# A pinned order for the projection's first half, later reads in the v stage and a later norm broadcast in an fp32 encoder on one core

## The chip, the core and the metric

The kernel runs on one core of a Trainium2 chip. The metric is the device time of one execution in microseconds (us), the median of several. The core has TensorE (PE: matmuls, and weight loads shown apart as PEld), VectorE (DVE), ScalarE (ACT), GpSimd (POOL) and SyncE (SP), which here issues DMAs. Each engine takes its instructions in order and waits on semaphores for the others. PSUM, into which PE writes, has eight banks of 128 x 512 fp32. The profile gives PE's granted clock as a share of full speed.

## The reference

An encoder trunk of 1024 tokens by 1024 channels in fp32, with two layers. Layer 0 mixes tokens by attention (16 query heads, 4 key/value heads of 64, with RMS-normalised and rotated queries and keys), layer 1 by a gated spatial unit (gMLP). Each layer ends in an MLP with a squared ReLU. Every part is normalised and modulated by a condition vector:

```python
for i in range(DEPTH):
    mod = cond @ ada_w[i] + ada_b[i]
    sh1, sc1, g1, sh2, sc2, g2 = jnp.split(mod, N_MOD, axis=-1)
    h = modulate(rmsnorm(x, norm1_g[i]), sh1, sc1)
    y = gqa_attention(h, ...) if i % 2 == 0 else chunked_gmlp(h, ...)
    x = x + g1[:, None, :] * y
    h = modulate(rmsnorm(x, norm2_g[i]), sh2, sc2)
    x = x + g2[:, None, :] * sq_relu_mlp(h, mlp_w_in[i], mlp_w_out[i])
```

with `modulate(h, s, c) = h * (1 + c) + s`. In the attention, `qkv = h @ w_qkv`, then the norm and the rotation of q and k, then a softmax per block of 128 queries.

## The kernel before

**Numbers.** Every fp32 operand of a large product is split in a high part (rounded to the engine's fast fp32 format, by ScalarE) and a low part (the difference, by VectorE or GpSimd). A product is then three matmuls: high by high, high by low, low by high. "A split" below is such a pair.

**Head, and the projection of the first 512 tokens.** `x` is held transposed, as eight tiles of 128 channels by 512 tokens (k = 0 to 7) for each half of the tokens. The head broadcasts the condition vector over the partitions by two products (`cb`), sums the squares of the eight tiles (ScalarE squares, VectorE adds), and contracts the sum over the partitions by four narrow products (`ss`, L269). From it `ms` (L271) and a reciprocal root on GpSimd (`r`) are made; `norm_rb` puts the root on a diagonal and multiplies it with ones (`rb`, L284), which broadcasts it over the partitions. Meanwhile the modulation is made for one channel tile at a time: `mod_load` loads a 128 x 1024 tile of `ada_w` and VectorE multiplies and sums it against the condition (L149). Shift and scale are two such tiles per k. `norm_u` multiplies x by scale and root (L293), `norm_hl` adds the shift and splits (L299 on ScalarE, L301 on VectorE).

The projection has three blocks of 512 output columns (cb 0: keys and values, cb 1 and cb 2: queries), with eight k each. `qkv_w(cb, kp, eng)` loads the weights for two k (512 KB), has ScalarE cast the high part (L544) and `eng` subtract the low part (L549). `qkv_mm(cb, kp, ...)` issues 12 matmuls for each k (L558 to L560), into four PSUM banks (two tiles of two banks, or four single banks). Blocks 0 and 1 run pair by pair in the order (0,0), (1,0), (0,1), (1,1), (0,2), (0,3), (1,2), (1,3), then block 2. Block 1's low parts for kp = 0 and block 2's for kp = 0 are made on GpSimd. A scheduler may move instructions where nothing holds them; `hold` keeps an instruction in program order while the flag `pinned` is set, and that is the case only for the first two k.

**Between the halves.** The norm of the second 512 tokens (`norm_rstd(sq1)`: ss, the root, rb) follows the third pair of block 2, with eight of its matmuls between ss and rb as scheduled. `norm_apply` then makes the eight splits of the second half (`hs1`). Keys are rotated and scaled in `k_rows`, which makes the sums of squares (`qk_sums`: square on ScalarE, reduce on VectorE, L606) and the reciprocal root (`qk_rstd`, which takes a square root on ScalarE) before the scaling; `q_sums` is the same for queries. Rotation (`qk_rope`, L616 to L619) reads block 2's banks directly for its queries, so that these banks are free only when it has read them. The second half runs block 0 (into four single banks), block 1 (into the two tiles of block 2 of the first half), then block 2; `kstacks` transposes the split keys on PE (L663).

**MLP and v stage.** The MLP's first product and the gMLP's value product (`wino_v`) use a seven-product scheme on 2 x 2 blocks. Its right operand (weights) and left operand (the normalised x) are combined into "forms", named 1, 2, 6, 5, 7, 3, 4 (`prep` for the weights of the v stage; `forms_b` for x of the second 512 tokens, L366 to L377), and each form is split (L318 and L319 for x, L1463 and L1464 for weights). The work goes in units of 12 matmuls; a callback `at(i)` after unit i issues a piece of other work. In `mlp`, `at` issues ss at unit HB, and rb and `forms_b` one unit later. In the v stage, q names the product and kt its four quarters; `done` reads the banks when a q is through (L1492); two sets of four banks alternate, q5 writing to the banks of q2. In `forms_b(..., apart=True)` the subtractions of the left operand are one step (`subtract`), issued as one run of eight (L377). `prep` makes q6 from three subtractions (L1458 to L1461), of which the third changes the block that q3 uses later.

## Time and profile before

| | |
|---|---|
| median of 3 runs | 2642.19 us (2641.83 to 2645.12) |
| profiled execution, its own time | 2640.55 us |
| its span, first to last instruction | 2638.8 us |
| PE busy | 2597.3 us, 98% |
| VectorE / ScalarE / GpSimd busy | 2183.3 / 1451.1 / 729.8 us |
| mean granted clock of PE | 0.997 |

In the rows shown later, a line of the timeline is start, duration, engine, source line, operation, output tile, input tiles, shape and count, with the idle time before it and the engine, tile and line that ended it in brackets. A row of the grouped waits is the waiting tile and line, the releaser, the total in us, the count, and the longest. Matmuls overlap, so that a matmul's own 0.39 us is longer than the distance to the next.

### The profile page before, as it was taken

To read this page: it belongs to the slowest core of one execution; us is meant where nothing else is said; L and a number is where in the kernel's file an instruction comes from. 1 tells how busy PE (TensorE), PEld (TensorE's weight loads), DVE (VectorE), ACT (ScalarE), POOL (GpSimd) and SP (SyncE) were. 2 spreads that over 40 slices of the span, in tenths; PEclk is the share of its full clock that TensorE was granted. 3 is DMA by queue.
4 is the path that set the end of the run, shared out by engine and by line. 5 is a ranking of instruction groups with operands and counts; after the bars stand their busy time and mean duration, and the time that the engine had idled before them with its cause. 6 is when DMAs were issued, how large, how long until landed. Compare 5 with 4: busy or idle time off the path is not lost. (4 is left out here: it accounts for less than half of the span.)

```text
span 2638.8 us, 37172 instructions
## 1 busy us (share of the span) xinstructions
PE 2597.3 (98%) x12788; PEld 2165.1 (82%) x12788; DVE 2183.3 (83%) x3271; ACT 1451.1 (55%) x2616; POOL 729.8 (28%) x535
## 2 busy tenths in 40 slices
PE   7999999999999999999999999999999999999999
PEld 5788999887788888888788888888888788888887
DVE  7868999887899989977886677788979977789974
ACT  4569999954654455446543444455456645465442
POOL 0238776533000004430122044551520000005400
PEclk9999999999999999999999999999999999999999
DMA  8110222234486788644243355558741554488461
GB/s 288 43 33 1 81 81 80 99 112 144 151 299 244 260 308 301 208 130 171 75 136 112 120 173 179 188 188 307 247 139 49 176 176 153 159 298 276 147 209 60
DMA packets 208751, 435.38 MB, mean 165 GB/s; under 512 B 23025, under 2 KB 35441, under 8 KB 208562
## 3 DMA queue, kind: packets, MB, share of 16 engines
q1 hardware_dynamic: 181682, 395.24, 44.2%
q10 hardware_dynamic: 26880, 37.76, 4.0%
q8 instruction: 101, 1.65, 0.3%
q14 instruction: 88, 0.72, 0.1%
HBM read 310.23 MB, written 122.68 MB: 164 GB/s over the span
## 5 line engine op out<-in xcount | busy, mean ns | idle before, releaser
L1171 PE MATMUL out<-t,s 128*128 128x512 f32 x1232 | 480.1, 390 | 1.4 <-ACT t L318 0.6
L1172 PE MATMUL out<-t,s 128*128 128x512 f32 x1232 | 479.5, 389 | 0.7 <-DVE t L319 0.7
L1173 PE MATMUL out<-t,s 128*128 128x512 f32 x1232 | 479.1, 389 | 0.0
L454 PE MATMUL w<-t,s 128*128 128x512 f32 x1168 | 459.8, 395 | 0.0
L455 PE MATMUL w<-t,s 128*128 128x512 f32 x1168 | 454.8, 390 | 1.5 <-DVE t L319 1.5
L456 PE MATMUL w<-t,s 128*128 128x512 f32 x1168 | 454.6, 389 | 0.0
L319 DVE TENSOR_TENSOR t<-t,t 128x512 fp32r<-128x512 f32 x408 | 329.5, 818 | 32.7 <-ACT t L318 22.4
L318 ACT CAST t<-t 128x512 fp32r<-128x512 f32 x408 | 244.7, 616 | 121.3 <-DMA t<-hf 64.0
L1171 PEld LDWEIGHTS out<-t,s 128*128 128x128 f32 x1232 | 231.2, 188 | 51.1 <-ACT t L318 2.1
L1172 PEld LDWEIGHTS out<-t,s 128*128 128x128 f32 x1232 | 231.2, 188 | 50.1 <-DVE t L319 1.8
L1173 PEld LDWEIGHTS out<-t,s 128*128 128x128 f32 x1232 | 231.2, 188 | 48.2
L439 ACT CAST s<-w 128x512 fp32r<-128x512 f32 x292 | 173.7, 616 | 162.2 <-PE w L456 107.4
L455 PEld LDWEIGHTS w<-t,s 128*128 128x128 f32 x1168 | 219.4, 188 | 48.4 <-DVE t L319 3.7
L454 PEld LDWEIGHTS w<-t,s 128*128 128x128 f32 x1168 | 219.3, 188 | 48.2 <-issue 3.5
L456 PEld LDWEIGHTS w<-t,s 128*128 128x128 f32 x1168 | 219.3, 188 | 45.5
L440 DVE TENSOR_TENSOR s<-w,s 128x512 fp32r<-128x512 f32 x292 | 220.8, 763 | 42.3 <-ACT s L439 41.7
L1153 ACT CAST s<-t 128x512 fp32r<-128x512 f32 x240 | 148.0, 621 | 193.3 <-PE out L1173 139.1
L1139 POOL TENSOR_TENSOR w<-w,t 128x512 f32<-128x512 f32 x20 | 32.4, 1622 | 775.7 <-DMA t<-hf 415.6
L1154 DVE TENSOR_TENSOR s<-t,s 128x512 fp32r<-128x512 f32 x240 | 193.7, 808 | 59.1 <-ACT s L1153 58.4
L910 DVE TENSOR_REDUCE mx<-s 128x1 f32<-128x1024 f32 x128 | 156.2, 1220 | 32.9 <-PE s L907 31.6
L933 DVE TENSOR_TENSOR t<-t,t 128x512 fp32r<-128x512 f32 x256 | 164.2, 682 | 15.9 <-ACT t L927 15.1
L943 PE MATMUL o<-t,t 128*128 128x256 f32 x1024 | 162.7, 291 | 0.0
(248 smaller groups left out, 5086.7 us busy)
## 6 DMA issues: line engine op xcount, KB each, us to landing
t<-hf SPq DMA_DIRECT2D x320, 256.0 KB, 3.7
hf<-c SPq DMA_DIRECT2D x156, 256.0 KB, 3.4
w<-in_wi_dram SPq DMA_DIRECT2D x64, 512.0 KB, 4.4
hf<-c ACTq DMA_DIRECT2D x96, 256.0 KB, 2.3
w<-in_ada_dram SPq DMA_DIRECT2D x36, 512.0 KB, 3.4
x<-in_ada_dram SPq DMA_DIRECT2D x64, 256.0 KB, 5.6
t<-in_wm_dram SPq DMA_DIRECT2D x64, 256.0 KB, 4.7
wf<-w SPq DMA_DIRECT2D x64, 256.0 KB, 2.9
```

The costliest lines, as they stand in the source:

```text
L318: S.copy(hi, src)
L319: (eng or V).tensor_tensor(lo, src, f32(hi), ALU.subtract)
L439: S.copy(hi, src)
L440: V.tensor_tensor(lo, src, f32(hi), ALU.subtract)
L454: T.matmul(ps, hi[:, a], th, start=kt == 0, stop=False)
L455: T.matmul(ps, hi[:, a], tl, start=False, stop=False)
L456: T.matmul(ps, lo[:, a], th, start=False, stop=kt == 3)
L933: pin(V.tensor_tensor(lo, pt, f32(hi), ALU.subtract))
L1154: V.tensor_tensor(lo, src, f32(hi), ALU.subtract)
L1171: T.matmul(ps, hi[:, a], th, start=begin and kt == 0, stop=False, **g)
L1172: T.matmul(ps, hi[:, a], tl, start=False, stop=False, **g)
L1173: T.matmul(ps, lo[:, a], th, start=False, stop=end and kt == 3, **g)
```

## The change

It has three parts.

1. **Head and first half.** `stay(n, src)` issues n products of a 128 x 128 block of ones with a 128 x 128 block of `src` into a bank that nobody reads (36 in all: before `cb`, after the squares of k = 2, 4 and 6, before and after `rb`). Everything from there to the second half's start stands in program order on PE, VectorE and ScalarE. The loop goes over single k, and for k below 6 multiplies block 0 and block 1 in turn; block 1's k = 6 and 7 follow later. All low parts of the first half's weights are made on VectorE. The loads of the modulation for k+1 are issued during k, into buffers named by `MT` (tag w or c). The second half's squares are spread over the first half; ss is issued in the middle of block 2's third pair, rb 24 matmuls later, with the diagonal made by one VectorE product. `k_rows` is divided: the rotation of the keys stands ahead of `norm_apply`; their sums, root and scaling (`k_scale`), and the sums and roots of block 1's queries, stand behind it. In the second half `k_scale` stands behind the first key transposes.
2. **MLP of layer 0.** rb and `forms_b` are issued two units after ss (`HR`), not one.
3. **v stage.** For the first third of the columns (p = 0) the third subtraction of q6 is put in a list and issued after unit 13, and the reads of q2's banks after units 9 to 11. The left operand's subtractions are divided between the forms 5 and 4, at whose split they are now made; the units at which pieces of `forms_b` are issued change, and the statistics begin after unit 15 instead of 13.

PE's order at the start of the program shows the unread products (`dm`). Before:

```order
1 L676 MATMUL cb_111<-c_91,ones 128x512
2 L676 MATMUL cb_113<-c_91,ones 128x512
3 L269 MATMUL ss_147<-ones,t_116 128x1 x4
4 L284 MATMUL rb_168<-t_156,ones 128x512
5 L558 MATMUL qkv_194<-s_160,t_174 128x512
```

With the change:

```order
1 L695 MATMUL dm_111<-ones 128x128 x10
2 L702 MATMUL cb_122<-c_91,ones 128x512
3 L702 MATMUL cb_124<-c_91,ones 128x512
4 L695 MATMUL dm_135<-t_132,ones 128x128 x6
5 L695 MATMUL dm_148<-t_145,ones 128x128 x6
6 L695 MATMUL dm_161<-t_158,ones 128x128 x4
7 L274 MATMUL ss_177<-ones,t_127 128x1 x4
8 L695 MATMUL dm_206<-ones 128x128 x6
9 L289 MATMUL rb_213<-t_186,ones 128x512
10 L695 MATMUL dm_215<-ones 128x128 x4
11 L575 MATMUL qkv_221<-s_190,t_229 128x512
```

Ten products stand ahead of `cb`, sixteen between `cb` and `ss`, and ten around `rb`; the order of what is read is the same.

VectorE's order behind `norm_apply` (its last row is L301, now L308), up to the first rotation that reads block 2's banks. Before:

```order
130 L301 SCALAR_TENSOR_TENSOR t_852<-t_844,mod,t_850 128x512
131 L606 TENSOR_REDUCE qss_906<-t_907 128x8
132 L606 TENSOR_REDUCE qss_906<-t_910 128x8
133 L606 TENSOR_REDUCE qss_906<-t_913 128x8
134 L606 TENSOR_REDUCE qss_906<-t_916 128x8
135 L616 TENSOR_TENSOR t_928<-qkv_631,t_553 128x512
```

With the change:

```order
120 L308 SCALAR_TENSOR_TENSOR t_863<-t_855,mod,t_861 128x512
121 L623 TENSOR_REDUCE qss_865<-t_866 128x8
123 L641 TENSOR_SCALAR qss_865<-qss_865 128x16
124 L246 RECIPROCAL y_874<-y_874 128x16
127 L250 SCALAR_TENSOR_TENSOR r_873<-e_877,y_874 128x16
128 L623 TENSOR_REDUCE qss_895<-t_896 128x8
132 L623 TENSOR_REDUCE qss_945<-t_946 128x8
135 L246 RECIPROCAL y_910<-y_910 128x32
138 L623 TENSOR_REDUCE qss_945<-t_955 128x8
139 L249 TENSOR_TENSOR e_913<-e_913,qss_895 128x32
140 L633 TENSOR_TENSOR t_967<-qkv_658,t_638 128x512
151 L635 TENSOR_TENSOR t_975<-qkv_658,t_640 128x8x32
```

Ten reduces (2 for the keys, 4 for block 1's queries, 4 for block 2's) and most of two reciprocal roots now stand where four reduces stood; the rotation of bank `qkv_658` begins at row 140, 20 rows after the last row of `norm_apply`, instead of 5.

VectorE's order in the v stage, around the last quarter of q6's form (`s_13960` before, `s_13992` now, is its low part). Before:

```order
1601 L1459 TENSOR_TENSOR x_13961<-c_13703,w_13691 128x512
1602 L367 TENSOR_TENSOR t_13953<-t_13179,t_13952 128x512
1603 L1460 TENSOR_TENSOR w_13695<-w_13695,x_13961 128x512
1604 L377 TENSOR_TENSOR t_13835<-t_13835,t_13029 128x512
1605 L377 TENSOR_TENSOR t_13239<-t_13239,t_13848 128x512
1606 L377 TENSOR_TENSOR t_13841<-t_13841,t_13079 128x512
1607 L377 TENSOR_TENSOR t_13302<-t_13302,t_13881 128x512
1608 L377 TENSOR_TENSOR t_13874<-t_13874,t_13130 128x512
1609 L319 TENSOR_TENSOR t_13957<-t_13953,t_13956 128x512
1610 L1464 TENSOR_TENSOR s_13960<-x_13961,s_13960 128x512
```

With the change:

```order
1594 L1500 TENSOR_TENSOR x_13993<-c_13742,w_13730 128x512
1595 L329 TENSOR_TENSOR t_13923<-t_13919,t_13922 128x512
1596 L334 TENSOR_TENSOR t_13944<-x_11679,t_13853 128x512
1597 L334 TENSOR_TENSOR t_13947<-x_11683,t_13853 128x512
1598 L376 TENSOR_TENSOR t_13950<-t_13915,t_13912 128x512
1599 L1508 TENSOR_TENSOR s_13992<-x_13993,s_13992 128x512
1600 L377 TENSOR_TENSOR t_13951<-t_13169,t_13950 128x512
1601 L1508 TENSOR_TENSOR s_14010<-c_13736,s_14010 128x512
1602 L1538 TENSOR_TENSOR x_13843<-v_13858,x_13843 128x512
```

The reads of q1's banks before this are rows 1566 to 1569 before and 1573 to 1576 now, so the low part has moved from 44 to 26 rows behind the first of them. The first read of q2's banks (`v_13858`) stands behind it, the fourth at row 1623.

The diff, cut to its core:

```diff
@@ -366,24 +376,29 @@
             V.tensor_tensor(t3[kt], b22[kt], b12[kt], ALU.subtract)
...
-            left.append((b12[kt], b11))
-            left.append((b21, t2))
+            left["5"].append((b12[kt], b11))
+            left["4"].append((b21, t2))
             if not apart:
-                subtract()
-
-        def subtract():
-            while left:
-                a, b = left.pop(0)
-                V.tensor_tensor(a, a, b, ALU.subtract)
...
+        def subtract(qs):
+            for q in qs:
+                while left[q]:
+                    a, b = left[q].pop(0)
+                    V.tensor_tensor(a, a, b, ALU.subtract)
...
-        left = []
-        return ([lambda kt=kt: forms(kt) for kt in range(4)] + [subtract] * apart
-                + [lambda q=q: later(q) for q in order])
+        def last(q):
+            if q in left:
+                subtract(q)
+            later(q)
+
+        left = {"5": [], "4": []}
+        return [lambda kt=kt: forms(kt) for kt in range(4)] + [lambda q=q: last(q) for q in order]
...
 
         def k_rows(hf, src):
-            kd = [qk_rope(src[j], 1, hf * 4 + 2 * j, 2) for j in range(2)]
+            return [qk_rope(src[j], 1, hf * 4 + 2 * j, 2) for j in range(2)]
+
+        def k_scale(kd, src):
             r = qk_rstd(qk_sums(src))
             for j in range(2):
                 qk_scale(kd[j], r, j)
-            return kd
 
         def k_split(kd):
             kk = []
...
+        def stay(n, src):
+            dm = bank_s("dm")
+            for _ in range(n):
+                hold(T.matmul(dm[:, :P], ones, src[:, :P], start=True, stop=True))
+
+        pinned[0] = True
+        stay(STAY[0], ones)
         cps = []
...
-        pinned[0] = True
         for k in range(KT):
-            sq0.add(xs[k])
+            sq = sq0.add(xs[k])
+            if k in (2, 4, 6):
+                stay(STAY[k // 2], sq)
...
-        next(w00)
-        mod_load(0, 0, 0, "w", False)
+        raw0 = qkv_hi(0, 0, True)
+        mr = {(0, 0): mod_raw(0, 0, 0, "w")[0]}
+        raw1 = qkv_hi(1, 0, False)
+        mod_load(0, 0, 0, "w", False, mr.pop((0, 0)))
+        stay(STAY[4], ones)
...
+        stay(STAY[5], ones)
         rb = slot()
...
+        hs = []
+
+        def first_h(k):
+
+            nonlocal raw0, raw1
+            kp, i = divmod(k, 2)
+            for j in (1, 0) if k else ():
+                mod_load(0, j, k, "", False, mr.pop((j, k)))
+            u = norm_u(xs[k], 0, 0, k, rb if k else rbp)
+            hi = norm_hi(u, 0, 0, k)
+            if k == 0:
+                hold(S.copy(rb, rbp))
+            if k < 7:
+                qkv_lo(0, kp, raw0, i, V)
+            if k and kp < 3:
+                qkv_lo(1, kp, raw1, i, V)
+            elif k == 6:
+                qkv_lo(0, kp, raw0, 1, V)
+            hs.append(norm_lo(u, hi, 0, 0, k))
+            if k == 0:
+                qkv_lo(1, kp, raw1, i, V)
...
+            if k < 7:
+                kp, i = divmod(k + 1, 2)
+                for j in (1, 0):
+                    mr[(j, k + 1)] = mod_raw(0, j, k + 1, MT[k + 1])[0]
                 if i == 0:
-                    qkv_w(0, kp, V, True)
-            for k in (2 * kp, 2 * kp + 1):
-                us.append(norm_u(xs[k], 0, 0, k, rb))
-            for i in range(2):
-                hs.append(norm_hl(us[i], 0, 0, 2 * kp + i))
-            pinned[0] = False
+                    raw0 = qkv_hi(0, kp, True)
+                    if kp < 3:
+                        raw1 = qkv_hi(1, kp, False)
+            else:
+                qkv_w(1, 3, V)
...
+        for k in range(KT):
+            if k == 6:
                 raw_tables = tables_load()
-            if (cb, kp) == (1, 2):
-                rk = k_copies(pk)
-                values(0, pk)
-                qkv_w(2, 0, G)
-            if (cb, kp) == (1, 3):
-                tables(*raw_tables)
-                kd = k_rows(0, rk)
-            qkv_mm(cb, kp, pq if cb else pk, hs)
+            first_h(k)
+            qkv_mm(0, k // 2, pk, hs, (k % 2,))
+            if k < 6:
+                qkv_mm(1, k // 2, pq, hs, (k % 2,))
...
+        qkv_w(2, 0, V)
+        values(0, pk)
+        rk = k_copies(pk)
+        qkv_mm(1, 3, pq, hs, (0,))
+        qkv_w(2, 1, V)
+        for k in range(2):
+            sq1.add(xs1[k])
+        tables(*raw_tables)
+        qkv_mm(1, 3, pq, hs, (1,))
         ps = banks(True)
-        qkv_w(2, 1, V)
         qkv_mm(2, 0, ps, hs)
...
+        qkv_w(2, 2, V)
+        for k in range(2, 5):
             sq1.add(xs1[k])
+        qkv_mm(2, 1, ps, hs)
+        qkv_w(2, 3, V)
+        for k in range(5, KT):
+            sq1.add(xs1[k])
+        qkv_mm(2, 2, ps, hs, (0,))
+        rbp = norm_ss(sq1, bank_x, True)
+        kd = k_rows(0, rk)
+        qkv_mm(2, 2, ps, hs, (1,))
+        qkv_mm(2, 3, ps, hs, (0,))
+        rb1 = norm_rb(rbp, bank_x)
+        hs1 = norm_apply(xs1, 0, 0, rb1)
+        k_scale(kd, rk)
+        qkv_mm(2, 3, ps, hs, (1,))
         rr = q_sums(r1)
...
+        pinned[0] = False
...
@@ -1340,9 +1381,9 @@
                     halves.step()
             if i == HB[layer]:
                 rest.append(norm_ss(sqs[0], bank_y))
-            elif i == HB[layer] + 1:
+            elif i == HB[layer] + HR[layer]:
                 rest[:] = forms_b(f, x[1], layer, 1, norm_rb(rest[0], bank_y, True), "5473")
-            elif i > HB[layer] and rest:
+            elif i > HB[layer] + HR[layer] and rest:
...
-                e.tensor_tensor(a12, a12, src, ALU.subtract)
+                if p:
+                    G.tensor_tensor(a12, a12, src, ALU.subtract)
+                else:
+                    third.append((a12, src))
...
+            dst = cur[to]
+
+            def read(j):
+                V.tensor_tensor(dst[j], ps[j], other[j], ALU.add)
+                if q in "2734":
+                    sink(dst[j], 2 * p + (q in "74"), j + 4 * (q in "73"))
...
+                if (p, q) == (0, "2"):
+                    waiting.append(lambda j=j: read(j))
+                else:
+                    read(j)
...
+            if waiting and i > 8:
+                waiting.pop(0)()
+                if i == 10:
+                    waiting.pop(0)()
+            if third and i > 13:
+                a12, src = third.pop(0)
+                V.tensor_tensor(a12, a12, src, ALU.subtract)
...
                 rest[:] = forms_b(f, x[1], 1, 0, norm_rb(rest[0], bank_y), "5734", True)
-            elif i > HBV + 2 and rest and (i <= HBV + 7 or i in (HBV + 8, HBV + 11, HBV + 15, HBV + 19)):
+            elif rest and i in (*range(HBV + 3, HBV + 7), 10, 12, 16, 20):
...
 
 SLOTS = {"t": 58, "x": 16, "w": 4, "s": 5}
 AHEAD = 1
-TL = (0, 3)
+STAY = (10, 6, 6, 4, 6, 4)
 LA = 3
 LAV = 3
-SD = 13
+MT = ("w", "w", "w", "w", "w", "c", "w", "c")
+SD = 15
 TA = 3
 FIRST = 6
 OUT_PRE = 6
@@ -1711,6 +1771,7 @@
 HK = 3
 LK = 4
 HB = (2, 1)
+HR = (2, 1)
 HBV = 1
```

More of the change, by code (lines that the diff above doesn't have):

```diff
@@ L141, in encoder_kernel, with mod_raw, mod_load @@
     cond = []
-    def mod_load(layer, j, k, tag="w", late=True):
+    def mod_raw(layer, j, k, tag):
         raw = wide(tag)
-        ld = nc.sync.dma_start(raw, t["ada"][layer, j * KT + k])
-        if tag == "w" and late:
-            pin(ld)
+        return raw, nc.sync.dma_start(raw, t["ada"][layer, j * KT + k])
+    def mod_load(layer, j, k, tag="w", late=True, raw=None):
+        if raw is None:
+            raw, ld = mod_raw(layer, j, k, tag)
+            if tag == "w" and late:
+                pin(ld)
         acc = mod[:, layer, j, k : k + 1]
@@ L268, in norm_ss @@
         for j in range(4):
-            T.matmul(ps[:, j : j + 1], acc[:, j * P : (j + 1) * P], ones[:, 0:1], start=True, stop=True)
+            hold(T.matmul(ps[:, j : j + 1], acc[:, j * P : (j + 1) * P], ones[:, 0:1], start=True, stop=True))
         ms = small.tile([P, 4], F32, tag="ms", name=nm("ms"))
@@ L283, in norm_rb @@
         ps = bank("rb")
-        T.matmul(ps, ones, dg, start=True, stop=True)
+        hold(T.matmul(ps, ones, dg, start=True, stop=True))
         if keep:
@@ L294, in norm_u, with norm_hi, norm_lo @@
         return u
[L296 to L302 removed]
+    def norm_hi(u, layer, which, k):
+        hi = slot(F32R)
+        hold(S.activation(hi, u, AF.Identity, bias=mod[:, layer, 3 * which, k : k + 1]))
+        return hi
+    def norm_lo(u, hi, layer, which, k):
+        lo = slot(F32R)
+        hold(V.scalar_tensor_tensor(lo, u, mod[:, layer, 3 * which, k : k + 1], f32(hi), ALU.add, ALU.subtract))
+        return hi, lo
+    def norm_hl(u, layer, which, k):
+        return norm_lo(u, norm_hi(u, layer, which, k), layer, which, k)
     def norm_apply(xt, layer, which, rb):
@@ L531, in qkv_w, with qkv_hi @@
         def qkv_w(cb, kp, eng, keep=False):
-            for f in qkv_w_steps(cb, kp, eng, keep):
-                pass
-        def qkv_w_steps(cb, kp, eng, keep):
+            raw = qkv_hi(cb, kp, keep)
+            for i in range(2):
+                qkv_lo(cb, kp, raw, i, eng)
+        def qkv_hi(cb, kp, keep):
             raw = wide("c", F32, (2, CB))
@@ L801, in encoder_kernel @@
         kstacks(0, kk, bank_x)
+        k_scale(kd, rk)
         kk = k_split(kd)
```

87 lines of the change are left out of this document (22 added, 65 removed).

## The prediction, as recorded before the changed kernel ran

> **What bounds the kernel now.** I read the busy shares first, then the waits of TensorE (PE) grouped by producer, then the clock in the windows around the longest waits.
>
> ```profile
> PE 2597.3 (98%) x12788; PEld 2165.1 (82%) x12788; DVE 2183.3 (83%) x3271; ACT 1451.1 (55%) x2616; POOL 729.8 (28%) x535
> ...
> PE qkv L558 <- ACT t L299: 5.7, 4, 3.0
> PE rb L284 <- ACT t L279: 3.7, 2, 2.9
> ...
> 20.40:61.00 40.60, 36.53 (x144) 28.77 (x145) 35.80 (x61) 13.97 (x29) 3.58 (x2) 0.96 0.77 265
> 37.00:40.50 3.50, 3.48 (x8) 2.59 (x9) 3.50 (x7) 2.69 (x5) 0.00 (x0) 0.52 0.59 211
> 661.80:665.20 3.40, 3.40 (x9) 2.31 (x8) 2.57 (x5) 1.85 (x3) 0.00 (x0) 0.50 0.00 0
> 683.00:700.00 17.00, 14.96 (x59) 10.08 (x58) 16.30 (x28) 12.91 (x25) 0.00 (x0) 1.00 0.42 145
> 1303.50:1310.30 6.80, 4.69 (x11) 3.20 (x12) 6.80 (x12) 2.89 (x6) 0.00 (x0) 0.50 0.00 0
> ```
>
> PE is busy 98% of the span, so nothing but its own idle time and its slow clock can be won. A group's row gives the wait in total, its count and its longest; a window's row gives its length, then busy time and instructions of PE, PEld, DVE, ACT and POOL, then the granted clock, the DMA share and GB/s. The longest waits (these two groups, and the rows further down with a bracket) sit in the places that the change touches: the head (ss, rb and the first products of the projection), the broadcast of the MLP's norm, and the v stage. Three of them are followed by some microseconds at half clock: 0.52 at 37.0, 0.50 at 661.8 and 0.50 at 1303.5. At that clock 11 matmuls took 4.69 us where 2.5 are normal (pitch below), a loss of 2.2 us beside the wait itself.
>
> **The head, first half of the tokens.**
>
> ```profile
> 3.30 3.78 PE L676 MATMUL cb<-c,ones 1*128 1x512 f32 x4 [3.30 <-ACT c L670]
> 12.73 1.87 PE L269 MATMUL ss<-ones,t 128*128 128x1 f32 x8 [5.65 <-DVE t L260]
> 16.68 2.08 PE L284 MATMUL rb<-t,ones 128*128 128x512 f32 x2 [2.09 <-DVE t L275]
> 20.42 0.79 PE L558 MATMUL qkv<-s,t 128*128 128x512 f32 x1 [1.66 <-ACT t L299]
> 37.02 0.72 PE L558 MATMUL qkv<-s,t 128*128 128x512 f32 x1 [3.03 <-ACT t L299]
> 84.51 0.50 PE L559 MATMUL qkv<-t,t 128*128 128x512 f32 x1 [0.78 <-DVE t L549]
> 90.31 0.95 PE L269 MATMUL ss<-ones,t 128*128 128x1 f32 x8
> 93.98 1.12 PE L284 MATMUL rb<-t,ones 128*128 128x512 f32 x2 [0.77 <-ACT t L279]
> ```
>
> The same ss takes 1.87 us at 12.73 and 0.95 at 90.31, the same rb 2.08 and 1.12: the first pair runs on a slow clock. If the 36 unread products keep the clock up, both are 1.9 us shorter in sum, and the first product of the projection starts at about 18.5 instead of 20.42. The products themselves stand in waits of 5.65, 2.09 and 1.66 us, in which PE has nothing else. No fp32 128x128 product is in the trace; the bounds for this term are 0 (they do not lift the clock) and 2.1.
>
> From 20.40 to 61.00 there are 144 matmuls. At the full pitch of 0.227 us (119.47 to 119.69 below) they need 32.7 of the 40.6 us: 7.9 us are lost to slow products at the start, to the 3.03 and to the half clock after it. In the new order a k serves both weight blocks: 24 matmuls, 5.44 us. VectorE's work for one k comes from these starts:
>
> ```profile
> 40.53 1.22 DVE L149 SCALAR_TENSOR_TENSOR w<-w,s 128x1024 f32<-128x1024 f32 x1
> 41.68 1.29 DVE L549 TENSOR_TENSOR w<-c,w 128x512 fp32r<-128x512 f32 x2
> 42.88 0.75 DVE L293 SCALAR_TENSOR_TENSOR t<-x,amod,t 128x512 f32<-128x512 f32 x1
> 43.54 1.22 DVE L149 SCALAR_TENSOR_TENSOR c<-c,s 128x1024 f32<-128x1024 f32 x1
> ```
>
> Two modulation products of 1.15, two low parts of weights at 0.60 each, L293 and L301 at 0.66 each, and some 0.13 for the small one: 5.0 to 5.1 us. So PE sets the pace up to k=5. At k=6 and 7 only the first block is multiplied, 2.72 us a k, against 5.0 and 3.8 on VectorE, which by then leads by about 2 us: it runs out by 1.1 us. With 0.3 and 0.35 for the low parts of k=0 and 1 this leaves 1.75 of the 7.9, a gain of 6.2. The two waits of 0.78 and 0.77 go as well (the low parts are made in time, and 24 matmuls stand between ss and rb instead of 8): 1.5. Head: 1.9+6.2+1.5 = **9.6 us** (bounds 5.4, with the clock still low through ss, rb and the first products, and 10).
>
> **What comes late instead: the second half.** The change puts the first half's key sums and query sums, behind norm_apply, ahead of the rope that reads the projection's last banks (cb 2).
>
> ```profile
> 95.76 1.42 DVE L293 SCALAR_TENSOR_TENSOR t<-x,amod,t 128x512 f32<-128x512 f32 x2 [4.30 <-ACT t L288]
> 108.39 2.46 DVE L606 TENSOR_REDUCE qss<-t 128x8 f32<-128x512 f32 x4
> 110.77 0.68 DVE L616 TENSOR_TENSOR t<-qkv,t 128x512 f32<-128x512 f32 x1
> 113.64 0.41 DVE L618 TENSOR_TENSOR t<-qkv,t 128x256 f32<-128x256 f32 x1
> 116.72 0.74 DVE L618 TENSOR_TENSOR t<-qkv,t 128x256 f32<-128x256 f32 x2
> ...
> 97.93 0.39 PE L558 MATMUL qkv<-s,t 128*128 128x512 f32 x1
> 119.47 0.39 PE L560 MATMUL qkv<-w,t 128*128 128x512 f32 x1
> 119.69 0.39 PE L558 MATMUL qkv<-t,t 128*128 128x512 f32 x1
> ...
> 1297.37 1.28 ACT L1470 ACT_TABLE_LOAD   x1
> ```
>
> PE starts the second half at 97.93 and comes to its second block of weights 21.8 us later, at 119.69; that block writes into the two tiles whose last reads are the L618 rows at 113.64 and 116.72. So there was slack of 5.7 and, as the second tile is wanted six matmuls later, 3.6 us. Now VectorE does six reduces more ((110.77-108.39)/4 = 0.60 each, 3.6 us) and the short rows of two more reciprocal roots (about 0.8 us each, partly between other rows). The first root cannot be had before ScalarE has squared five rows, loaded a table (1.28 at 1297.37, the same kind of load) and taken the root, some 4.5 us after the last L299, while VectorE has work for only 2: 2.5 us idle, with everything queued behind it. Together 7.7 us. Before, the tiles were free 18.3 and 21.7 us after norm_apply's start (95.76); now 26.0 and 29.4. PE is there at 97.93-95.76+21.8 = 24.0 and waits 2.0; six matmuls on, at 27.4, it waits for the second tile, 2.0 again. The key transposes behind it then wait little more, as the stalls have given VectorE the time. So 4.0 us (3.4 to 4.9, by how the short rows fall between the others), and 0.7 for a half-clock spell (two waits of 2.16 and 2.11 brought one in the v stage, a single of 0.78 did not). Cost **4.7 us**, bounds 0 (if the root's idle time finds cover and the rope starts as early as before) and 6.6.
>
> The Trainium skill ("TensorE: Matmul & The Clock Gate", Part 1) says that the clock falls after an idle window of about 3.4 us; by that these waits would cost their own length alone. The rows disagree: 2.88 and 3.03 us of idleness were enough here.
>
> **The MLP norm, layer 0.**
>
> ```profile
> 661.12 1.48 PE L284 MATMUL rb<-t,ones 128*128 128x512 f32 x2 [2.88 <-ACT t L279]
> 694.73 0.50 PE L455 MATMUL w<-t,s 128*128 128x512 f32 x1 [1.02 <-DVE t L319]
> ...
> 658.51 0.16 DVE L271 TENSOR_SCALAR ms<-ss 128x4 f32<-128x4 f32 x1
> 662.63 2.48 DVE L324 TENSOR_TENSOR t<-x,rb 128x512 f32<-128x512 f32 x4 [3.96 <-PE rb L284]
> ```
>
> Twelve more matmuls (2.72 us) ahead of rb fill the 2.88 us, and 1.5 us of half clock go with it: 4.4 in sum. But rb itself is not earlier, since its diagonal is made from ms at 658.51 as before, so the chain of forms on VectorE still begins near 662.6. That chain is the next bound: from 683 to 700 VectorE is busy 16.30 of 17 us, PE only 14.96, and PE already waits there for single forms (694.73). PE merely arrives sooner. Some 0.4 us come from rb at full clock, and about 0.9 from a subtraction and a sum that move into VectorE's idle 3.96 us. I take **1.3 us**; bounds 0.5 and 4.4.
>
> **The v stage.**
>
> ```profile
> 1303.32 1.54 PE L1517 MATMUL v<-s,t 128*128 128x512 f32 x3 [2.16 <-ACT s L1463]
> 1306.97 0.79 PE L1518 MATMUL v<-s,t 128*128 128x512 f32 x1 [2.11 <-DVE s L1464]
> ...
> 1302.62 3.09 DVE L377 TENSOR_TENSOR t<-t,t 128x512 f32<-128x512 f32 x5
> 1306.23 0.68 DVE L1464 TENSOR_TENSOR s<-x,s 128x512 fp32r<-128x512 f32 x1
> ```
>
> The last form of q6 and its low part (L1464 at 1306.23) stand behind five subtractions of the left operand (3.09 us). In the new order that low part is 18 VectorE rows earlier, 18 x 0.60 = 10.8 us, and would be done near 1296, 5 us ahead of its use. The two waits and the half clock, 2.16+2.11+2.2 = 6.5, go. What is late next: the reads of q2's banks, deferred over 28 rows, set free the last bank near 1310.5, while q5 wants it near 1311.2. VectorE is saturated there, and a slip by one row is a wait. I allow 0.9 for this and for ScalarE's queue: **5.6 us**, bounds 2.5 and 6.5.
>
> **Sum.** 9.6 - 4.7 + 1.3 + 5.6 = 11.8 us against the profiled execution: 2640.55 - 11.8 = 2628.75. The runs' median, 2642.19, lies 1.6 above that execution, so I say 2629.
>
> **The rivals.**
> - Everything hidden as meant. The rope's slack holds (0 instead of 4.7), and forms_b follows rb for 4.4: 9.6+4.4+6.2 = 20.2, 2620 to 2621. For it: the pinned order puts all else early. Against: 16.30 of 17 us, and the six reduces. Chance 0.14.
> - The clock stays low in the head, as the unread products are thin bursts between waits: first product at 20.4, slow products until about 23.5 again, 4.2 us less, 2633. For it: cb at 3.30 kept PE busy for 3.78 us, and ss at 12.73 was slow all the same, though with 5.65 us of idleness between. Chance 0.16. The Trainium skill (same page and part) has such a rule: full rate needs a window of about 3.4 us that is busy throughout, and half rate is the default; no row here shows a partly filled window.
> - The new waits eat the gain: 6.6 in the second half with half clock, q5's banks late by two rows with half clock (v only 2.5), cold head (5.4), MLP 0.5: 1.8 gained, 2639. Chance 0.13.
> - Slower: the loads of a k come on the path. SP issues in order, and a load that waits for its buffer holds all behind it.
>
> ```profile
> c<-in_wqkv_dram SPq DMA_DIRECT2D x9, 512.0 KB, 5.0
> c<-in_ada_dram SPq DMA_DIRECT2D x4, 512.0 KB, 5.7
> ```
>
>   In the new order k=5 and 7 take c buffers that the low parts two k's before set free, and k=6's weights wait for k=5's. If the lead is one pass short, each of k=4 to 7 pays most of its landing, 5.4 us, 21.6 in sum: 2650. It decides from 3 us a k on. Against: by the order the buffers are free about 6 us before the need, and 1.5 MB in 5.44 us is 290 GB/s, where the window moved 265 at 0.77 share. Chance 0.07.
>
> **How the numbers follow.** My own case has 0.50 and spans 2624 to 2633. About 0.2% (5.3 us) is what a measurement of this kernel can tell from no change. All of the first two rivals and my case lie beyond it on the fast side (0.80); of the third about a tenth does too, so faster is 0.81, with 0.12 for no difference and 0.07 for slower. The range reaches from the first rival to the middle of the third: 2620 to 2637.
>
> **What would show it.** Right: first product of the projection near 18.5; no wait above 1.2 us until the second half; a wait on a VectorE rope at its second block; no half clock near the MLP's rb, yet longer waits on L319's successor 20 to 35 us later; no wait above 1 us at q6. Wrong: a 0.5 clock row past 20 us in the head, no wait at the second block, or waits on DMA in the k loop.

## The result, and the profile after

The changed kernel takes 2626.51 us (median of 4 runs, 2625.21 to 2627.54) where the kernel before takes 2642.64 us (4 runs, 2641.83 to 2645.12). The ratio is 0.9937, with a 95% interval of 0.992 to 0.9954: some 16 us faster. The forecast was 2629 us, in a range of 2620 to 2637. Between the two profiled executions, 2640.55 and 2627.54 us, the gain is 13.0 us against 11.8 in the sum. The executions of one kernel differ by 3 us and more, for reasons that come out below, so the terms are best compared instruction by instruction.

Where the time went is read from the starts of the same PE instructions in the two traces (before minus after):

| place | before | after | earlier by | gained since the row above | forecast |
|---|---|---|---|---|---|
| first product of the projection | 20.42 | 19.45 | 0.97 | 1.0 | 1.9 |
| first product of the second half | 97.93 | 89.47 | 8.46 | 7.5 | 7.7 |
| second key transposes | 145.21 | 140.37 | 4.84 | -3.6 | -4.7 |
| ss of layer 0's MLP | 654.31 | 651.31 | 3.00 | -1.8 | 0 |
| ss of layer 1's first norm | 1190.57 | 1183.85 | 6.72 | 3.7 | 1.3 |
| first product behind the v stage (w, L454, now L469) | 1506.52 | 1492.95 | 13.57 | 6.9 | 5.6 |
| end of the span | 2638.8 | 2625.8 | 13.0 | -0.6 | 0 |

The waits of PE, grouped by what waits and what ends it (total, count, longest), in the changed kernel:

```profile
PE t L965 <- DVE t L974: 2.9, 4, 1.1
PE t L965 <- ACT c L957: 2.4, 3, 1.9
PE qkv L575 <- DVE t L635: 2.1, 1, 2.1
PE w L470 <- DVE t L329: 1.8, 6, 0.5
PE w L469 <- ACT t L328: 1.7, 2, 1.2
PE qkv L575 <- ACT t L303: 1.2, 2, 0.8
...
PE rb L289 <- ACT t L284: 0.2, 1, 0.2
```

The projection's waits on L299 (5.7 us in total before) and the wait of ss (5.65) have shrunk to 1.2 and 0.8, those of rb on ScalarE from 3.7 to 0.2, and the v stage's are gone; the longest that is left on the changed path is new, the 2.1 us on a rotation (L635). In windows (length, busy time and instructions of PE, PEld, DVE, ACT and POOL, then the granted clock):

```profile
115.10:118.50 3.40, 3.40 (x10) 2.63 (x9) 3.40 (x5) 0.11 (x1) 3.24 (x4) 0.50 0.00 0
500.80:504.20 3.40, 3.40 (x14) 2.91 (x13) 1.39 (x3) 3.39 (x7) 3.40 (x7) 0.50 0.46 119
678.00:694.00 16.00, 13.67 (x49) 8.42 (x49) 15.78 (x28) 11.37 (x22) 0.00 (x0) 1.00 0.44 147
1293.00:1310.00 17.00, 17.00 (x75) 13.75 (x74) 17.00 (x29) 10.71 (x20) 0.00 (x0) 1.00 0.46 138
```

Half clock at 37, 662 and 1303 us is gone; instead there are two spells of 3.4 us, at 115 behind the new wait and at 501 in the attention. From 678 to 694 PE still waits for VectorE's forms. From 1293 to 1310, where the v stage lost its 6.5 us, PE is busy for the whole 17 us, and so is VectorE.

The head on PE, with the unread products (`dm`), and the new wait:

```profile
1.04 4.63 PE L695 MATMUL dm<-ones 128*128 128x128 f32 x20 [1.04 <-DVE mhalf L99]
5.60 2.08 PE L702 MATMUL cb<-c,ones 1*128 1x512 f32 x4
13.29 1.05 PE L274 MATMUL ss<-ones,t 128*128 128x1 f32 x8 [0.75 <-DVE t L264]
16.66 1.12 PE L289 MATMUL rb<-t,ones 128*128 128x512 f32 x2 [0.88 <-DVE t L280]
19.45 0.50 PE L575 MATMUL qkv<-s,t 128*128 128x512 f32 x1 [0.77 <-ACT t L303]
...
113.59 0.47 PE L575 MATMUL qkv<-t,t 128*128 128x512 f32 x1 [2.11 <-DVE t L635]
```

The same four records of cb take 2.08 us behind the first ten unread products and took 3.78 before: the clock is up from 5.6 us on. (The granted clock that the profile shows is no help here: it stands at 1.00 from the start in every trace, also where ss took 1.87 us before the change. So at the start the clock is read from the durations.) The first products push cb back by 2.3 us (it began at 3.30), which costs nothing in this execution, since ss waits 0.75 us for the squares. In two others it does cost (see the head below).

### The profile page after: what moved, and what is told of

It is laid out like the page before. It is cut to its first block, busy times and chain, and to the rows that moved or that the text cites. A ratio compares the mean times of both kernels' runs of the same rounds, so it can differ in the third digit from the quotient of the medians.

```text
span 2625.8 us, 37307 instructions
## 1 busy us (share of the span) xinstructions
PE 2601.6 (99%) x12860; PEld 2172.2 (83%) x12860; DVE 2183.1 (83%) x3276; ACT 1451.1 (55%) x2612; POOL 723.2 (28%) x531
## 5 line engine op out<-in xcount | busy, mean ns | idle before, releaser
L469 PE MATMUL w<-t,s 128*128 128x512 f32 x1168 | 459.8, 395 | 0.9 <-ACT t L328 0.5
L454 ACT CAST s<-w 128x512 fp32r<-128x512 f32 x292 | 173.4, 616 | 161.4 <-PE w L471 104.3
L469 PEld LDWEIGHTS w<-t,s 128*128 128x128 f32 x1168 | 219.3, 188 | 49.4 <-issue 2.9
```

Source lines behind the costliest of these rows:

```text
L454: S.copy(hi, src)
L469: T.matmul(ps, hi[:, a], th, start=kt == 0, stop=False)
```

## The experiments

Each kernel was timed in five rounds beside the kernel before (2643.4 us in the first group, e0 to e3; 2643.85 in the second, e4 to e6 and e0b). The changed kernel ran in both groups.

**The changed kernel again (e0, e0b).** No edit.

> The changed kernel again, as the yardstick for the three that follow. Expected 2625 to 2628 us, with the same waits: 2.1 us at the second half's second weight block with 3.4 us of half clock after it. Open is the wait of 1.9 us near 498 us in the attention (ScalarE's cast of the output weights waited for their load there): if it is a chance of that execution's loads, it is about 0.6 us here, as before the change, and the half clock after it is absent; if it belongs to the change, it is 1.5 to 2 us again.

> The changed kernel once more as the yardstick on this chip: 2625 to 2627 us. What varies by chance between its executions should be the start (first product of the projection between 18.9 and 20.9 us, with the landing of x) and the half clock after the attention's wait near 498 us.

2626.20 us (ratio 0.9931, 0.9919 to 0.9943) and 2627.03 us (0.9937, 0.9925 to 0.995). Second block and first key transposes on PE, of e0:

```profile
112.85 0.47 PE L575 MATMUL qkv<-t,t 128*128 128x512 f32 x1 [2.11 <-DVE t L635]
125.58 3.23 PE L681 MATMUL kt<-identr,t 128*128 128x128 f32 x32 [1.57 <-DVE t L611]
```

The wait of 2.1 us is in every execution, but half clock followed it only in the first one (e1's clock record shows no spells at all). In e0 there was none behind it; a second wait of 1.57 us stands at the key transposes instead (1.60 in e0b), which the first trace does not have. The sum is the same, 3.7 us: VectorE sets the time of the transposes, and PE loses its 1.6 us either in slow products or in a wait. The attention's wait, which I had left open, did not vanish: 1.25 and 0.61 in e0, 0.80 and 0.63 in e0b, 1.89 in one in the first trace, 0.61 and 0.62 before. The half clock behind it did in e0.

**No unread products (e1).**

```diff
-STAY = (10, 6, 6, 4, 6, 4)
+STAY = (0, 0, 0, 0, 0, 0)
```

> Only the 36 unread products are left out; the pinned order stays. My theory: they are worth the faster rb (1 us) and full-rate first products (about 2.3 us), so the first product starts near 20.4 instead of 19.45, the first dozen products run at half rate, and the second half's first product comes 2.5 to 3.5 us later; since VectorE is then further ahead, the wait at the second weight block does not change, and the time is 2628.5 to 2630. Rival: the pinned order alone does the work, the clock comes up by itself within the first products and VectorE sets the pace: less than 1 us, 2626 to 2627.5.

2627.97 us (0.994, 0.9927 to 0.9952), 1.8 us above e0, between the two. The intervals of e0 and e1 overlap, so the trace has to carry this. Its head on PE:

```profile
13.29 1.87 PE L274 MATMUL ss<-ones,t 128*128 128x1 f32 x8 [6.26 <-DVE t L264]
17.24 2.08 PE L289 MATMUL rb<-t,ones 128*128 128x512 f32 x2 [2.08 <-DVE t L280]
20.98 0.79 PE L575 MATMUL qkv<-s,t 128*128 128x512 f32 x1 [1.66 <-ACT t L303]
```

ss starts at 13.29 in both this and the first trace of the changed kernel, so the two heads compare directly: without the products ss and rb take their slow 1.87 and 2.08 us, and the first product starts 1.53 us later (20.98, 19.45). The slow products behind it put PE back by 1.6 us more (the 25th starts at 28.52, in the first trace at 25.36), but that is regained at k = 6 and 7, where the changed kernel's PE waits for the other engines: PE reaches the second block's wait 1.6 us later than there (113.10 and 111.48). There the other engines set the pace, as the rival said; at rb they do not. The profile gives a clock of 0.95 for this execution from 25 us on, yet from the first product to the second half it takes 70.1 us against 70.0; that record is not used here.

**The v stage as before (e2), and alone (e6).** e2 takes back the five pieces of the v stage, e6 makes only them in the kernel before. The core of e2:

```diff
-                if p:
-                    G.tensor_tensor(a12, a12, src, ALU.subtract)
-                else:
-                    third.append((a12, src))
+                e.tensor_tensor(a12, a12, src, ALU.subtract)
...
-                if (p, q) == (0, "2"):
-                    waiting.append(lambda j=j: read(j))
-                else:
-                    read(j)
+                V.tensor_tensor(cur[to][j], ps[j], other[j], ALU.add)
```

> The v stage as before the change (third subtraction and q2's reads in place, the left operand's eight subtractions in one run, statistics after unit 13); all else changed. My theory: the two waits of 2.2 and 2.1 us at the last quarter of q6 and the 6.8 us of half clock come back and nothing else moves: 6.5 to 7 us slower than the changed kernel, 2632.5 to 2634. Rival: part of the gain came from the earlier arrival of the norm or from other reshuffles in that stage, so that undoing it gives back less than 4 us.

> The kernel before with the v stage's part alone (deferred third subtraction and reads of q2, subtractions at the forms 5 and 4, statistics after unit 15). If the parts are independent: 6.5 to 7 us faster than the kernel before, 2635.5 to 2637, with no wait above 0.5 us between 1290 and 1315. If the v stage needs the earlier arrival that the other parts give, some of the two waits of 2.1 us remain and it gains less than 4 us.

e2 took 2633.23 us (0.996, 0.9948 to 0.9973), 7.0 above e0; e6 2633.38 us (0.9965, 0.9952 to 0.9977), 10.5 below its kernel before by the medians. In e2's trace both waits are back:

```profile
1300.71 1.65 PE L1553 MATMUL v<-s,t 128*128 128x512 f32 x3 [2.20 <-ACT s L1499]
1304.36 0.80 PE L1554 MATMUL v<-s,t 128*128 128x512 f32 x1 [2.00 <-DVE s L1500]
```

Compared by the same instructions, from the v stage's first product to the first one behind it, the changed kernel takes 230.6 us, e2 237.3, the kernel before 237.4 and e6 230.6: e2 loses 6.7 us and e6 gains 6.8. So the part is worth the same with and without the others; no wait above 0.3 us is left where the two stood. Which of its five pieces does how much, no run separates. The profiled execution of e6 lies 7.2 us below that of the kernel before (2633.31 and 2640.55), nearly all of it from the 6.8 in the v stage and a first product that came 0.8 us earlier. The rest of the 10.5 us is in the yardstick: the kernel before had a median of 2643.85 us in that group, 3.3 above that execution.

**Query sums later (e3).**

```diff
         qkv_mm(2, 3, ps, hs, (1,))
-        rr = q_sums(r1)
         pinned[0] = False
...
         kstacks(0, kk, bank_x)
+        rr = q_sums(r1)
         k_scale(kd, rk)
```

> The sums and roots of the first half's queries (four reduces of 0.6 us and a root) are moved behind the first key transposes of the second half; the key sums stay. My theory: VectorE reaches the rotation that frees the second block's banks 3 to 5 us sooner, the wait of 2.1 us and the half clock after it (1.6 us) both go, and the time falls by 3.5 us to 2622 to 2624. Rival: VectorE is the bound of the whole stretch, so that the wait comes back at the key transposes or at the rotation that needs these sums (1 to 3 us there), and less than 1.5 us are won.

2632.92 us (0.9953, 0.9939 to 0.9966): 6.7 us slower than e0, a miss, and worse than the rival; its runs are wide (2627.40 to 2635.92). The wait at the second block is gone, but PE now waits at the transposes. PE, then ScalarE:

```profile
129.07 1.17 PE L681 MATMUL kt<-identr,t 128*128 128x128 f32 x8 [3.32 <-ACT x L683]
...
127.40 1.15 ACT L622 ACTIVATE t<-t 128x512 f32<-128x512 f32 x2 [4.33 <-DVE t L633]
128.45 3.97 ACT L683 CAST x<-kt 128x512 fp32r<-128x512 f32 x8
```

The moved squares (L622) wait 4.33 us for VectorE, and ScalarE's copies of the transposes (L683), which set the transpose banks free, stand behind them. The second transposes wait 1.91 us in the same way, and half clock follows both. Work moved out of the way of one wait was put in front of another. By the same instructions that costs 4.7 us between the second half's first product and its last (83.6 us, 78.9 in e0). Not all of the 6.7 belongs to the edit: in the profiled execution the head was 2.0 us later than e0's, because its clock came up late (below).

**Both sums ahead of norm_apply (e4).** Sums and roots of the keys and of block 1's queries stand between ss and rb, the key rotation behind norm_apply:

```diff
+        ssk = qk_sums(rk)
         qkv_mm(2, 2, ps, hs, (0,))
         rbp = norm_ss(sq1, bank_x, True)
-        kd = k_rows(0, rk)
+        ssq = qk_sums(r1)
+        rstd = [qk_root(ss) for ss in (ssk, ssq)]
+        kr, rr = [f() for f in rstd]
...
         hs1 = norm_apply(xs1, 0, 0, rb1)
-        k_scale(kd, rk)
+        kd = k_rows(0, rk)
+        for j in range(2):
+            qk_scale(kd[j], kr, j)
         qkv_mm(2, 3, ps, hs, (1,))
-        rr = q_sums(r1)
```

`qk_root` is `qk_rstd` with both square roots issued ahead of the VectorE rows that use them, in pinned order.

> The key and query sums and both roots stand before the second half's norm_apply (where ScalarE has 11 us and VectorE 2 us idle), the key rotation behind it: VectorE has 4.0 us of extra work between norm_apply and the rotation that frees the banks, not 7.7 with an idle spell. My theory (VectorE's queue bounds that stretch, and only taking work out of it helps): banks free at 22.3 and 25.7 us after norm_apply's start against PE's 24.0 and 27.4, so no wait at the second weight block, a rest of 0 to 1 us at the key transposes, and 2.5 to 3.5 us less than the changed kernel: 2622.5 to 2624. Rival: ScalarE's copies or the key split at the transposes bound it as they did with the query sums moved back, and the wait only moves: 2625.5 to 2627.5.

2623.47 us (0.9924, 0.9912 to 0.9937): 3.6 us below e0b, as expected, and 20.4 below the kernel before. VectorE's reduces and norm_apply, then PE:

```profile
77.20 1.27 DVE L623 TENSOR_REDUCE qss<-t 128x8 f32<-128x512 f32 x2
81.35 2.46 DVE L623 TENSOR_REDUCE qss<-t 128x8 f32<-128x512 f32 x4
86.59 1.41 DVE L298 SCALAR_TENSOR_TENSOR t<-x,amod,t 128x512 f32<-128x512 f32 x2 [0.60 <-ACT t L293]
...
122.67 3.23 PE L698 MATMUL kt<-identr,t 128*128 128x128 f32 x32 [1.00 <-DVE t L611]
```

The six reduces fill time in which VectorE waited for ss and rb, norm_apply starts when rb is there, and the only wait between 84 and 135 us is 1.00 at the transposes. The changed kernel loses 3.7 us there, this one 1.0. From the second half's first product to the second key transposes it takes 48.2 us, the changed kernel 50.9 and the kernel before 47.3, so 2.7 of the 3.6 us are shown to be the edit's.

**The MLP norm one unit after ss (e5).**

```diff
-HR = (2, 1)
+HR = (1, 1)
```

> Only the MLP's rb and forms_b go back to one unit behind ss in layer 0. My theory now (after the trace: VectorE's chain had 2 us of idle time that the later rb lets it use, so most of the 4.4 us came through): the wait of 2.9 us at rb and the 3.4 us of half clock come back, the waits between 680 and 690 us do not shrink, and the time is 3 to 4 us above the changed kernel, 2629 to 2630.5. The rival is my recorded term: VectorE bounds the forms anyway, so only 1 to 1.5 us come back, 2627 to 2628.

2631.75 us (0.9954, 0.994 to 0.9967), 4.7 above e0b, a little more than expected; its runs are wide (2627.69 to 2636.78). By the same instructions it loses 3.2 us from the MLP's ss to the ss of layer 1's first norm (535.8 us, 532.5 to 532.6 in three executions of the changed kernel, 536.3 before). PE, and the clock behind rb:

```profile
657.02 2.08 PE L289 MATMUL rb<-t,ones 128*128 128x512 f32 x2 [2.90 <-ACT t L284]
690.46 0.50 PE L470 MATMUL w<-t,s 128*128 128x512 f32 x1 [1.01 <-DVE t L329]
...
656.60:660.00 3.40, 2.98 (x5) 1.76 (x6) 0.87 (x2) 0.98 (x4) 0.00 (x0) 0.50 0.00 0
```

So the recorded 1.3 us was too small.

## Why the prediction was right, point by point

**Right in the whole.** 2626.5 lies in the range, 2.5 us from the forecast; the terms have the right signs, and that the sum came so near is partly luck, as their errors cancel: head 1.1 too high, second half 1.1 too dear, MLP 2.4 and v stage 1.3 too low, the attention not foreseen. There is also a slip in the sum: 2628.75 is the forecast for the profiled execution, and with the 1.6 us by which the median lay above it I should have said 2630.4. By the medians the gain is 16.1 us, by the profiled executions 13.0, against 11.8.

**The head, 9.6 forecast, 8.5 measured.** The step from the first product on was close (7.7 and 7.5). The term for the unread products, 1.9, was mis-sized: 0.97 between the two traces, 1.5 by e1, where ss starts at the same time. Part of the 1.9 was taken back in VectorE's queue: ms stands behind the first modulation product, so that of the 0.82 us of the faster ss only 0.57 come through (from ss to ms 1.33 us, 1.90 in e1). The other 0.56 between the two traces is the landing of x: the sum of the squares ended at 13.24 us after the change and at 12.68 before. I had also written that the trace holds no fp32 product of 128x128, so that only bounds could be given. The key transposes are of that form (`kt`, 16 records in 1.50 us before the change); the unread products took 12 records in 1.58 us.

The rival of a head that stays at half clock fell in five of the seven traces with these products, where cb took 1.98 or 2.08 us. In e2 and e3 its first half came true: the first product is later than the 20.4 us that the rival had, though the products behind it run at full rate. PE in e2, and VectorE's last additions of squares there:

```profile
5.60 3.78 PE L697 MATMUL cb<-c,ones 1*128 1x512 f32 x4
9.31 5.97 PE L690 MATMUL dm<-t,ones 128*128 128x128 f32 x32
15.12 0.95 PE L274 MATMUL ss<-ones,t 128*128 128x1 f32 x8
...
8.70 3.88 DVE L264 TENSOR_TENSOR t<-t,t 128x512 f32<-128x512 f32 x5 [1.50 <-ACT t L260]
```

cb is as slow as before the change, and the 32 records of unread products behind it take 5.97 us (12 in 1.60 and 20 in 2.50 in the first trace). The squares are summed at 12.58, but ss stands behind the unread products until 15.12; in e3 it is 11.45 and 15.05. Their first products start at 20.95 and 20.87 us, in the other five traces at 18.49 to 19.45. By the sum of the squares (13.23 in e1, whose first product starts at 20.98) I estimate that without the unread products they would have started near 20.3 and 19.2. So the products won some 1.5 us where the clock came up, and lost 0.6 and 1.7 us where it did not.

No run takes back the new order of the first half alone, or its parts singly. That the 7.5 us behind the first product belong to it rests on the traces: to the second half's first product it takes 77.5 us in the two with the old order (before, e6) and 69.5 to 71.5 in the eight with the new one.

**The second half, 4.7 forecast, 3.6 measured.** This step named the place, the producer and nearly the size. In the changed kernel:

```profile
87.53 1.41 DVE L298 SCALAR_TENSOR_TENSOR t<-x,amod,t 128x512 f32<-128x512 f32 x2 [1.11 <-ACT t L293]
...
103.35 0.25 DVE L246 RECIPROCAL y<-y 128x16 f32<-128x16 f32 x1 [1.60 <-ACT y L245]
...
113.03 0.41 DVE L635 TENSOR_TENSOR t<-qkv,t 128x256 f32<-128x256 f32 x1
...
115.22 0.74 DVE L635 TENSOR_TENSOR t<-qkv,t 128x256 f32<-128x256 f32 x2
```

The first tile is free 25.9 us after norm_apply's start (forecast 26.0) and PE waits 2.11 us (2.0). That it fits to a tenth is partly luck: VectorE's idle spell for the first root is 1.60 us, not 2.5, and of the 7.6 us added the six reduces leave 2.4 to the short rows, not 1.6. The second wait of 2.0 us did not come: PE's built order multiplies two k into the first tile before it touches the second. I had taken source order there, by which the seventh product would write to the second tile; it started at 115.05 without a wait, though that tile's last read ended at 115.96. What I set at "little more", the transposes, took 1.6 us of wait in its place in e0, e0b, e1, e2 and e5; in the first trace the half clock at 115 us had used up that time. e4 shows the cause: with VectorE's work elsewhere, 2.7 of the 3.7 us go. Sums that are merely moved back do not help, as e3 shows.

**The MLP norm, 1.3 forecast, 3.7 measured.** The wait at rb went as said (2.88 to 0.17). The step that failed is "that chain is the next bound". VectorE was close to full, but its chain of forms had holes of its own, each behind another engine or a load. Before:

```profile
668.49 1.29 DVE L319 TENSOR_TENSOR t<-t,t 128x512 fp32r<-128x512 f32 x2 [0.84 <-ACT t L318]
672.09 0.69 DVE L462 TENSOR_TENSOR c<-w,c 128x512 f32<-128x512 f32 x1 [0.51 <-PE w L456]
693.38 0.69 DVE L432 TENSOR_TENSOR w<-w 128x512 f32<-128x512 f32 x1 [0.70 <-DMA w<-in_wi_dram]
```

After, one hole of 0.22 us is left, and the idle time ahead of the chain is 2.94, not 3.96 us:

```profile
658.61 0.69 DVE L329 TENSOR_TENSOR t<-t,t 128x512 fp32r<-128x512 f32 x1 [2.94 <-ACT t L328]
687.35 0.69 DVE L483 TENSOR_TENSOR c<-w,c 128x512 f32<-128x512 f32 x1 [0.22 <-PE w L471]
```

That is 2.9 us of VectorE time; I had counted 1.3. The waits of PE on forms between 680 and 692 us stayed at some 2.3 us (2.0 before), where I forecast that they would grow by 3. What the clock alone does, e6 tells: there rb stands where it stood before and waits 2.92 us, but no half clock follows. VectorE in e6:

```profile
660.61 2.48 DVE L324 TENSOR_TENSOR t<-x,rb 128x512 f32<-128x512 f32 x4 [3.61 <-PE rb L284]
668.78 0.69 DVE L467 TENSOR_TENSOR c<-w,c 128x512 f32<-128x512 f32 x1 [0.16 <-PE w L461]
```

The hole of 0.84 us is gone, those of 3.96 and 0.51 are smaller, and the one of 0.70 behind the load stays (0.69). By the same instructions PE in e6 is 1.6 us ahead of the kernel before from the end of that half clock on (it loses that again near 1056 us, where ScalarE waits 2.55 us for a load of `hf`), the changed kernel 3.4 to 3.7. So, by this one execution, some 1.6 us of the 3.7 come from the absent half clock and 2.1 from the later rb itself.

**The v stage, 5.6 forecast, 6.9 measured.** The mechanism is confirmed by e2 and e6. My allowance of 0.9 for q2's banks and ScalarE was not needed: VectorE is busy for all of the 17 us from 1293 on, and still every deferred read is in time: no wait follows at q5.

**The attention, not forecast, -1.8.** Its work is the same. ScalarE casts the output weights ahead of a softmax row, and their load did not come earlier by as much as the rest. After, then before:

```profile
497.85 1.05 ACT L116 CAST s<-w 128x1024 fp32r<-128x1024 f32 x1 [2.27 <-DMA w<-in_wo_dram]
...
501.48 1.05 ACT L116 CAST s<-w 128x1024 fp32r<-128x1024 f32 x1 [1.01 <-DMA w<-in_wo_dram]
```

PE stood 1.89 us behind it, and 3.4 us of half clock followed. With the 0.6 us of the row behind it, the wait comes to between 1.1 and 2.0 us in all runs but e6 (0.63); half clock came at it in some, and at the 16 narrow products some 15 us earlier in others (below). The sum is 1.23 before, and 1.89, 1.86 and 1.43 in three executions of the changed kernel. From the second key transposes to the MLP's ss the kernel before takes 509.1 us and e6 508.3; the seven executions with the change's first part, e3 left out, take 510.3 to 512.5. That points to this part rather than to chance; which step of it makes the wait longer stays open.

**The rivals.** "All hidden as meant" (2620) failed by the second half's 3.6 us, and e4, which takes most of that away, comes out at 2623.5. The rival of the late loads came true in small: waits on DMA in the k loop, which I had named as a sign of being wrong, are there at k = 7, one of the two k that it named. VectorE after the change, and in e2:

```profile
53.30 1.23 DVE L153 SCALAR_TENSOR_TENSOR c<-c,s 128x1024 f32<-128x1024 f32 x1 [0.68 <-DMA c<-in_ada_dram]
...
56.50 1.22 DVE L153 SCALAR_TENSOR_TENSOR c<-c,s 128x1024 f32<-128x1024 f32 x1 [2.38 <-DMA c<-in_ada_dram]
```

VectorE waits for this load in six of the eight traces, 0.3 to 2.4 us, and PE behind it 0.40 us after the change, 1.01 in e0b and 2.09 in e2, where 21.6 was priced. After the change PE is busy for all but 0.55 us from 19.4 to 64 us.

## What to carry to other kernels

When waits are taken out of an in-order program, follow the engine behind the next deadline row by row in its built order, not in source order: the first wait on the rotation was forecast so (2.0 us, 2.11 measured), the second, read from the source, did not exist. Work without an early consumer belongs where its engine is idle for want of another result (the sums between ss and rb won 2.7 us by the same instructions), not merely further down the queue, where it stood ahead of other copies and lost 4.7. And an engine that is busy for 16.3 of 17 us need not bound its chain: ask what its idle tenths wait for, and whether that goes with the wait that is taken out.

## What the runs showed of the hardware

- **Half clock after a wait does not come every time.** The same wait of 2.9 us at the MLP's rb was followed by 3.4 us of half clock in the kernel before and in e5, and by none in e6; rb took 1.48 and 2.08 us in the former and 1.13 in the latter. The 2.1 us wait at the second block brought half clock in one execution of the changed kernel and none in e0, e0b, e2 and e5. Other spells stand where no long wait is: in e0b one began at 485.6 us, behind 3.60 us in which PE was busy for 3.50, but with transposes and 16 products of a single column (am, 128x1); e2, e3 and e4 have one near the same place. A spell inside the program lasts 3.4 us or 6.8 in every trace that has one. e6 around rb, granted clock 1.00 throughout, and e0b around the spell in the attention:

```profile
659.44 1.13 PE L284 MATMUL rb<-t,ones 128*128 128x512 f32 x2 [2.92 <-ACT t L279]
...
656.50:663.00 6.50, 3.58 (x15) 2.64 (x15) 2.89 (x6) 3.42 (x8) 1.01 (x1) 1.00 0.00 0
```

```profile
483.52 1.95 PE L209 MATMUL am<-ones,s 128*128 128x1 f32 x16
...
482.00:485.60 3.60, 3.50 (x31) 3.23 (x30) 2.16 (x5) 3.41 (x9) 0.55 (x1) 1.00 0.00 0
485.60:489.00 3.40, 3.40 (x16) 3.07 (x15) 1.46 (x3) 0.14 (x1) 0.17 (x1) 0.50 0.00 0
```

  The Trainium skill ("TensorE: Matmul & The Clock Gate", Part 1) says that activity is watched in windows of about 3.4 us that run free of the program. The lengths of the spells, and that they come in one execution and not in the next, agree with that. For the fall of the clock it names an idle window of that length, and here the traces differ: no wait ahead of a spell was longer than 3.32 us (e3, at the transposes), the other long ones were 1.9 to 3.0, and PE was busy for most of the window at 482. In the prediction I charged the spells as certain where they had been seen once.
- **Products that nobody reads lift the clock, but not at a time one can count on.** Ten fp32 products of 128x128 on an otherwise empty PE (20 records, 3.83 to 4.64 us) had it at full rate by the end of cb in five of seven traces. In the first trace, bursts with idle time of about 0.8 us between them kept it there through ss and rb; in e0, e0b, e4 and e5 a spell of half clock fell between 7.3 and 12.3 us and was over before rb. In e2 and e3 PE was busy from 1.04 us on and still slow until past 13: in e2 it ran 18 records in the 3.7 us from 9.3 to 13.0, and 21 in the 2.0 us from 14 to 16.
- **A start that varies by 2.5 us.** With the same head, the first product of the projection began between 18.49 and 20.95 us. Up to 1.8 us of that is the landing of x (the sum of the squares ended at 11.45 to 13.24 us); the two latest starts are those at slow clock, of which one, e3, had the earliest x of all. How much of the spread between the executions without a trace this makes is not shown.
